# Seven-product tile: ScalarE's four PSUM copies ordered ahead of its casts of later weights

## The chip, the cores and the metric

The kernel runs on one core of one Trainium2 chip. The metric is the device time of one execution in microseconds. Five engines work side by side, each through its own list of instructions in order: TensorE (PE in the profile; its weight loads are shown apart as PEld), VectorE (DVE), ScalarE (ACT), GpSimd (POOL) and SyncE (SP). They wait for each other through semaphores.

## What is computed

The reference is one decoder layer on 512 tokens of width 1024, in float32: a gated feed-forward part, three token mixers (sparse attention, gated delta rule, cross-attention into a memory) whose gated sum is projected, and a second feed-forward part. Cut to what matters here:

```
def swiglu(x, w_gate, w_up, w_down):
    return (jax.nn.silu(x @ w_gate) * (x @ w_up)) @ w_down
...
h = swiglu(rms_norm(x, ffn1_pre_norm[l]), ffn1_w_gate[l], ffn1_w_up[l], ffn1_w_down[l])
x = x + 0.5 * rms_norm(h, ffn1_post_norm[l])
...
gates = jax.nn.sigmoid(u @ w_branch_gate[l]).reshape(b, s, N_BRANCH, d)
merged = (gates[:, :, 0] * (o_nsa @ w_branch_nsa[l]) + gates[:, :, 1] * (o_dn @ w_branch_dn[l]) + gates[:, :, 2] * (o_mem @ w_branch_mem[l]))
...
h = swiglu(rms_norm(x, ffn2_pre_norm[l]), ffn2_w_gate[l], ffn2_w_up[l], ffn2_w_down[l])
```

The feed-forward width is 2816, which makes 22 tiles of 128 features in each feed-forward part.

## The kernel before

**Split products.** A float32 operand is kept as a high part (a cast, on ScalarE) and a low part (operand minus high part, on VectorE). One product is three matmuls: high by high, low by high, high by low.

**The seven-product tile.** One tile needs two products of the same tokens, gate and up, 128 features by 512 tokens each, over 1024 inputs. Seen as a 2 by 2 block matrix (gate and up; two halves of the inputs) times a 2 by 2 block matrix (two halves of the inputs; two halves of the tokens), it takes seven block products in place of eight, at the price of sums of weights and of tokens made beforehand. `fast_prods` (line 469) makes one tile. A block product (`prod`, line 476) is 12 matmuls of 128x256, all from line 482. The seven go into four PSUM banks, called a, q7, g and u in the code. In the profile the banks carry the names smm, so or sr, se, ss in the feed-forward tiles and de, ds, dmm, do in the merge tiles.

**The four copies.** Several results share a partial sum, so ScalarE copies a bank while the tile goes on: after the first product a to the left half of g (line 488), after the third minus a to u (line 493), after the fourth q7 to SBUF (s7, line 495), and after the fifth a to the right half of g (line 497). The third product accumulates on a, so it may not start before the copy of line 488 has read a; the fifth product stands in the same way behind line 493. The names of the seven-product weights S and tokens T pick the block sums. VectorE then makes `up` from s7, a and u (lines 502 and 503), ScalarE the silu of g (line 466) and VectorE the product (line 467).

**The weights of the next tiles.** `fast_load` (line 421) brings the four quarters of a later tile's gate and up weights in by four DMAs on SyncE's queue (tile fq), makes their three sums on VectorE (line 428, tiles fs and fq), seven casts on ScalarE (lines 434 and 441) and the low parts on VectorE (lines 437 and 442). The high and low parts are fset for one set and fxth, fxtl for the other; the sets alternate from tile to tile. The merge has one set (mset, from mfq and msum).

**Where tiles run.** `fast_phase` (line 507) runs 17 tiles in the first feed-forward part (from 75 to 239 us) and 18 in the second (from 1000 to 1173 us). Seven more run in the merge of the mixers (from 774 to 897 us), where cross-attention (lines 1341 to 1361, tiles pms, pmt, pmo) and the products of the branches (pfm) are mixed in. So there are 42 tiles and 168 copies. Beside them ScalarE and VectorE split weights of the down projection ahead of time (line 106 to whi, line 109 to wlo, loaded into wraw by line 105).

**What sets the order.** A scheduler puts every engine's instructions into one fixed list when the kernel is built. It follows priorities, which by default are the order in which the code issues the instructions, and its own estimate of when each can start. `self.tc.high_priority(offset=n)` issues the instructions inside as if they stood n places earlier. Engines then run their lists strictly as written.

Of the kernel before, what the change touches and what calls it, by code (L numbers as in the profile page):

```python
# [14 lines left out]
AF = mybir.ActivationFunctionType  # L15
# [24 lines left out]
class Body:  # L40
# [428 lines left out]
    def fast_prods(self, S, T, banks, s7, mid=()):  # L469

        nc, v, te = self.nc, self.nc.vector, self.nc.tensor
        hi, lo = S
        a, q7, g, u = banks
        a, q7, u = a[:, :256], q7[:, :256], u[:, :256]

        def prod(out, w, t, start=False):
            th, tl = T[t]
            for k in range(4):
                c = slice(k * P, k * P + P)
                wh, wl = hi[:, w, c], lo[:, w, c]  # L480
                n = (k // 2, k % 2) if len(th.shape) == 4 else (k,)
                m = lambda x, y, **kw: te.matmul(out, x, y, skip_group_check=True, **kw)  # L482
                m(wh, th[:, *n], start=start and k == 0, stop=False)
                m(wl, th[:, *n], start=False, stop=False)
                self.tick(m(wh, tl[:, *n], start=False, stop=k == 3), 3 * 256)

        prod(a, self.S_A11, self.T_B11, True)
        nc.scalar.copy(g[:, :256], a)  # L488
        prod(q7, self.S_S3, self.T_T3, True)
        for f in mid[:1]:  # L490
            f()
        prod(a, self.S_S2, self.T_T2)
        nc.scalar.activation(u, a, AF.Copy, scale=-1.0)  # L493
        prod(g[:, :256], self.S_A12, self.T_B21)
        nc.scalar.copy(s7, q7)
        prod(a, self.S_S1, self.T_T1)
        nc.scalar.copy(g[:, 256:], a)  # L497
        prod(u, self.S_A22, self.T_T4)
        for f in mid[1:]:
            f()  # L500
        up = self.tp.tile([P, SEQ], F32, tag="tmpb", bufs=2, name="up")
        v.tensor_tensor(up[:, 256:], s7, a, op=OP.subtract)  # L502
        v.tensor_tensor(up[:, :256], u, s7, op=OP.add)
        prod(g[:, 256:], self.S_S4, self.T_B22)
        return g, up
# [1379 lines left out]
```

## Time and profile before

| | |
|---|---|
| median of 3 runs | 1288.67 us (1288.58 to 1291.4) |
| profiled execution | 1287.24 us |
| its span | 1285.5 us |
| PE busy | 1260.4 us (98%) |
| PEld busy | 1104.8 us (86%) |
| DVE busy | 982.4 us (76%) |
| ACT busy | 733.1 us (57%) |
| granted PE clock | 0.996 of full speed |

A row of the timeline begins with its start and its length in us, then engine, line, operation, output and inputs (buffer numbers left out), and a count where equal instructions follow each other. In brackets stands how long the engine had been idle before and what ended that. A matmul's length is modelled and overlaps the next one; the distance between starts is what counts.

### The profile page before, as it was taken

The numbers are of one execution on the slowest core, as the hardware profiler recorded it, in microseconds if no ns is written. First come the engines' busy times: TensorE is split into PE (matmuls) and PEld (weight loads), VectorE is DVE, ScalarE is ACT, GpSimd is POOL, SyncE is SP. The second block draws the span as 40 slices with busy tenths as digits, with TensorE's granted clock in tenths as the row PEclk, the third lists the DMA queues.
The fourth block names the chain that finished last, engine by engine and source line by source line (L and its number), as shares of the span: only waits on it lengthen the run. The fifth ranks groups of instructions, "written<-read, shape, count | busy, mean of one in ns | idle before, by whom it ended". The sixth has DMA issues, their size and how long they took to land.

```text
span 1285.5 us, 21909 instructions
## 1 busy us (share of the span) xinstructions
PE 1260.4 (98%) x8067; PEld 1104.8 (86%) x8067; DVE 982.4 (76%) x1769; ACT 733.1 (57%) x1487; POOL 209.1 (16%) x224
## 2 busy tenths in 40 slices
PE   8999999999999999999999999999999999999997
PEld 7899999888787778888777778899788999999886
DVE  6898787698967866755789766564797988786988
ACT  6556665675755644415565545553676766655663
POOL 0011112130002222102221112132200121110300
PEclk9999999999999999999999999999999999999999
DMA  6567756894753341233211142132853687664963
GB/s 221 173 200 178 181 165 129 244 210 172 239 186 106 104 125 57 83 111 115 74 58 58 42 146 76 60 112 71 295 192 105 216 183 193 186 130 161 229 224 115
DMA packets 109244, 190.38 MB, mean 148 GB/s; under 512 B 18653, under 2 KB 28241, under 8 KB 109137
## 3 DMA queue, kind: packets, MB, share of 16 engines
q1 hardware_dynamic: 92976, 154.12, 37.2%
q0 software_dynamic: 15872, 34.61, 13.9%
q8 instruction: 63, 1.03, 0.3%
q14 instruction: 45, 0.36, 0.1%
q10 hardware_dynamic: 288, 0.26, 0.1%
HBM read 178.90 MB, written 33.08 MB: 165 GB/s over the span
## 4 chain that ended last, share of the span: by engine, by line
PE 84%; DVE 6%; issue 4%; DMA 3%; ACT 2%; POOL 1%; SPq 0%; ACTq 0%; DVEq 0%; POOLq 0%
PE smm L482 11%; PE se L482 7%; PE acc_mm L712 7%; PE pfm L117 5%; PE pfm L118 5%; PE pfm L119 5%; PE acc_s L712 4%; PE ss L482 4%; PE de L482 2%; PE sr L482 2%; PE ps L1292 2%; PE so L482 2%; PE dmm L482 2%; PE po L1328 1%; PE ppt L1314 1%
## 5 line engine op out<-in xcount | busy, mean ns | idle before, releaser
L106 ACT CAST whi<-wraw 128x512 fp32r<-128x512 f32 (+1 forms) x174 | 105.2, 612 | 108.9 <-PE pfm L119 63.9
L109 DVE TENSOR_TENSOR wlo<-wraw,whi 128x512 fp32r<-128x512 f32 (+1 forms) x142 | 97.3, 694 | 36.3 <-ACT whi L106 34.9
L575 POOL DMA_DIRECT2D T<-in_ffn_d_dram x88 | 59.5, 677 | 380.3 <-PE pg L119 110.7
L118 PE MATMUL pfm<-xth,wlo 128*128 128x512 f32 x272 | 109.0, 406 | 1.3 <-POOL wlo L109 1.3
L117 PE MATMUL pfm<-xth,whi 128*128 128x512 f32 x272 | 108.5, 404 | 1.5 <-ACT whi L106 0.6
L119 PE MATMUL pfm<-xtl,whi 128*128 128x512 f32 x272 | 108.2, 403 | 0.0
L482 PE MATMUL smm<-thi,fset 128*128 128x256 f32 x432 | 76.7, 277 | 0.7 <-ACT ss L493 0.4
L109 POOL TENSOR_TENSOR wlo<-wraw,whi 128x512 fp32r<-128x512 f32 x29 | 39.4, 1361 | 219.7 <-ACT whi L106 165.1
L482 PEld LDWEIGHTS smm<-thi,fset 128*128 128x128 f32 x432 | 65.2, 188 | 1.5 <-ACT se L488 0.7
L502 DVE TENSOR_TENSOR up<-s,smm 128x256 f32<-128x256 f32 x35 | 14.7, 421 | 63.5 <-ACT se L497 63.5
L117 PEld LDWEIGHTS pfm<-xth,whi 128*128 128x128 f32 x272 | 51.2, 189 | 12.3 <-ACT whi L106 1.0
L118 PEld LDWEIGHTS pfm<-xth,wlo 128*128 128x128 f32 x272 | 51.2, 189 | 10.7 <-POOL wlo L109 1.8
L694 ACT CAST ringh<-ringr 128x1024 fp32r<-128x1024 f32 (+1 forms) x44 | 45.1, 1032 | 25.6 <-PE acc_mm L712 7.3
L119 PEld LDWEIGHTS pfm<-xtl,whi 128*128 128x128 f32 x272 | 51.1, 189 | 9.1 <-issue 0.4
L482 PE MATMUL smm<-thi,fxth 128*128 128x256 f32 x204 | 56.3, 276 | 0.0
L482 PE MATMUL smm<-thi,fxtl 128*128 128x256 f32 x204 | 56.3, 276 | 0.0
L482 PE MATMUL se<-thi,fset 128*128 128x256 f32 x288 | 50.9, 276 | 0.0
L727 DVE TENSOR_TENSOR sl<-H,sh 128x1024 fp32r<-128x1024 f32 (+2 forms) x38 | 40.9, 1080 | 4.1 <-ACT sh L726 4.1
L1295 ACT ACTIVATE Pm<-Pm,nm 128x384 f32<-128x384 f32 (+2 forms) x64 | 35.6, 558 | 14.6 <-DVE nm L1294 14.1
L482 PEld LDWEIGHTS se<-thi,fset 128*128 128x128 f32 x288 | 43.4, 188 | 0.0
L428 DVE TENSOR_TENSOR fs<-fq 128x1024 f32<-128x1024 f32 x35 | 43.2, 1233 | 0.0
L712 PE MATMUL acc_mm<-ringh,sh 128*128 128x512 f32 x108 | 42.2, 391 | 0.0
(640 smaller groups left out, 4375.1 us busy)
## 6 DMA issues: line engine op xcount, KB each, us to landing
T<-in_ffn_d_dram POOLq DMA_DIRECT2D x88, 256.0 KB, 4.1
fq<-in_ffn_g_dram SPq DMA_DIRECT2D x70, 256.0 KB, 3.3
fq<-in_ffn_u_dram SPq DMA_DIRECT2D x70, 256.0 KB, 4.0
wraw<-in_ffn_d_dram SPq DMA_DIRECT2D x34, 256.0 KB, 3.7
ringr<-T SPq DMA_DIRECT2D x16, 512.0 KB, 5.0
ringr<-in_ffn_d_dram POOLq DMA_DIRECT2D x16, 512.0 KB, 8.2
woraw<-in_w_out_dram SPq DMA_DIRECT2D x32, 256.0 KB, 3.6
mfq<-in_w_gate_dram SPq DMA_DIRECT2D x28, 256.0 KB, 3.1
```

The costliest lines, as they stand in the source:

```text
L106: nc.scalar.copy(hi, raw)
L109: self.lmark = eng.tensor_tensor(lo, raw, hi.bitcast(F32), op=OP.subtract)
L117: t.matmul(out, lh, rh, start=first, stop=False)
L118: t.matmul(out, ll, rh, start=False, stop=False)
L119: self.tick(t.matmul(out, lh, rl, start=False, stop=last), 3 * math.prod(out.shape[1:]))
L428: add = lambda *x: v.tensor_tensor(*x, op=OP.add)
L482: m = lambda x, y, **kw: te.matmul(out, x, y, skip_group_check=True, **kw)
L575: i = g.dma_start(o[c], x[c], max_dma_last_dim=2048, **({"accum_op": OP.add} if add else {}))
L694: nc.scalar.copy(hi, raw)
L712: e = lambda a, b, s, f: nc.tensor.matmul(acc[i], a, b, start=s, stop=f, skip_group_check=True)
L727: last = tt(low, f, hi.bitcast(F32), op=OP.subtract)
L1295: nc.scalar.activation(pm, pm, AF.Exp, bias=nm[:, qb : qb + 1], scale=-1.0, accum_out=sm[:, qb : qb + 1])
```

## The change

The four copies are issued through a helper that raises their priority by 100 places. Nothing else is altered.

```
+        def first(f, *x, **k):
+            with self.tc.high_priority(offset=100):
+                f(*x, **k)
+
         prod(a, self.S_A11, self.T_B11, True)
-        nc.scalar.copy(g[:, :256], a)
+        first(nc.scalar.copy, g[:, :256], a)
         prod(q7, self.S_S3, self.T_T3, True)
...
         prod(a, self.S_S2, self.T_T2)
-        nc.scalar.activation(u, a, AF.Copy, scale=-1.0)
+        first(nc.scalar.activation, u, a, AF.Copy, scale=-1.0)
         prod(g[:, :256], self.S_A12, self.T_B21)
-        nc.scalar.copy(s7, q7)
+        first(nc.scalar.copy, s7, q7)
         prod(a, self.S_S1, self.T_T1)
-        nc.scalar.copy(g[:, 256:], a)
+        first(nc.scalar.copy, g[:, 256:], a)
```

All four copies now carry the line of the helper's call, 489, and lines behind them are four higher than before. The lists that the scheduler makes are the same but for a few rows. Three places follow.

ScalarE at the first tile of the first feed-forward part, where se is the bank g, smm the bank a, and fxth the casts for the second tile. Before:

```order
L434 CAST fxth<-fq_750 128x512 x3
L441 CAST fxth<-fs 128x512 x2
L441 CAST fxth<-fq_750 128x512
L488 COPY se<-smm 128x256
L495 COPY s_752<-so 128x256
```

And now:

```order
L434 CAST fxth<-fq_750 128x512 x3
L441 CAST fxth<-fs 128x512
L489 COPY se<-smm 128x256
L441 CAST fxth<-fs 128x512
L441 CAST fxth<-fq_750 128x512
L489 COPY s_752<-so 128x256
```

The copy has moved ahead of two casts. On PE, two matmuls of the second tile that stood between the second and the third product of the first tile have gone back to the second tile; and the first tile of the second feed-forward part has its copy ahead of one cast (the second of the two fs) in the same way.

ScalarE in the second tile of the first feed-forward part, from the silu of the first tile on; ss is the bank u. Before:

```order
L466 ACTIVATE sg<-se 128x512
L488 COPY se<-smm 128x256
L434 CAST fxth<-fq_750 128x512
L495 COPY s_753<-sr 128x256
L441 CAST fset<-fq_749 128x512
L493 ACTIVATE ss<-smm 128x256
L441 CAST fxth<-fs 128x512
```

And now:

```order
L466 ACTIVATE sg<-se 128x512
L489 COPY se<-smm 128x256
L434 CAST fxth<-fq_750 128x512
L489 COPY s_753<-sr 128x256
L441 CAST fset<-fq_749 128x512
L441 CAST fxth<-fs 128x512
L489 ACTIVATE ss<-smm 128x256
```

The copy of minus a to u has moved behind one cast.

VectorE at the end of the first tile and in the second; wlo is the low part of a weight of the down projection. Before:

```order
L502 TENSOR_TENSOR up<-s_752,smm 128x256
L109 TENSOR_TENSOR wlo<-wraw,whi 128x512
L442 TENSOR_TENSOR fset<-fs,fset 128x1024
L503 TENSOR_TENSOR up<-ss,s_752 128x256
L437 TENSOR_TENSOR fset<-fq_749,fset 128x1536
L467 TENSOR_TENSOR H<-sg,up 128x512
L428 TENSOR_TENSOR fq_749<-fq_749 128x512
L428 TENSOR_TENSOR fs<-fq_750 128x1024
L442 TENSOR_TENSOR fset<-fq_749,fset 128x1024
L428 TENSOR_TENSOR fq_750<-fs,fq_750 128x512
L502 TENSOR_TENSOR up<-s_753,smm 128x256
```

And now:

```order
L506 TENSOR_TENSOR up<-s_752,smm 128x256
L442 TENSOR_TENSOR fset<-fs,fset 128x1024
L507 TENSOR_TENSOR up<-ss,s_752 128x256
L437 TENSOR_TENSOR fset<-fq_749,fset 128x1536
L467 TENSOR_TENSOR H<-sg,up 128x512
L428 TENSOR_TENSOR fq_749<-fq_749 128x512
L428 TENSOR_TENSOR fs<-fq_750 128x1024
L442 TENSOR_TENSOR fset<-fq_749,fset 128x1024
L428 TENSOR_TENSOR fq_750<-fs,fq_750 128x512
L109 TENSOR_TENSOR wlo<-wraw,whi 128x512
L506 TENSOR_TENSOR up<-s_753,smm 128x256
```

The subtraction wlo has moved back by eight rows. On SyncE's queue the next load of wraw, which needs the buffer that it frees, stands behind four loads of fq now and stood ahead of them before. In the merge, one copy of line 488 stands ahead of one cast, one copy of line 495 behind the cast omth of line 131, and at a few places PE takes tile matmuls and attention matmuls in another alternation. All other rows of all engines stand as before.

## The prediction

> **What bounds the kernel now.** I read the page first, then the list of waits for TensorE (PE) and its weight loads (PEld), then busy time by stage, and last the timeline at the few places where the changed order differs. The page says that PE is busy nearly all of the span:
>
> ```profile
> PE 1260.4 (98%) x8067; PEld 1104.8 (86%) x8067; DVE 982.4 (76%) x1769; ACT 733.1 (57%) x1487; POOL 209.1 (16%) x224
> ```
>
> The change can only help where PE waits for one of the four copies (lines 488, 493, 495, 497). The first two rows are of PE's waits over the whole span, the third of its weight loads between 995 and 1173 us:
>
> ```profile
> PE smm L482 <- ACT ss L493: 0.4, 1, 0.4
> PE smm L482 <- ACT se L488: 0.3, 1, 0.3
> PEld smm L482 <- ACT se L488: 0.2, 1, 0.2
> ```
>
> The columns are total us, times, longest. So 168 copies (four in each of 42 tiles) cost PE three waits. Everywhere else PE does not stop. Busy time by stage (span of the stretch, PE, PEld, DVE, ACT, POOL, clock, DMA share, GB/s), for steady tiles of the first feed-forward part and for the merge:
>
> ```profile
> 92.00:140.00 48.00, 48.00 (x424) 48.00 (x423) 38.62 (x45) 29.91 (x62) 8.45 (x12) 1.00 0.73 176
> 774.00:900.00 126.00, 125.98 (x839) 112.94 (x838) 75.40 (x108) 63.37 (x138) 33.96 (x22) 1.00 0.25 80
> ```
>
> Here a rule has to be weighed. The Trainium skill (Perfetto Trace Analysis, Identifying the Most-Contended Engine) says that matmul occupancy is a bad measure and that weight-load occupancy should be used. By the whole-span PEld figure 14%, about 180 us, would then be open to gain. In the tile stage the trace has 48.00 of 48.00 us for PEld as well, so applied stage by stage the rule leaves nothing there either, and the sum below goes by the three waits.
>
> **The change part by part.** Nothing is added or removed: the same instructions in another order. Of the 168 copies three come earlier by one or two casts, two come later by one, and 163 stand where they stood. I take the places in order of time.
>
> **First tile of feed-forward 1.** PE, around the wait:
>
> ```profile
> 77.12 0.40 PE L482 MATMUL so<-thi,fset 128*128 128x256 f32 x2
> 77.35 0.28 PE L482 MATMUL so<-tmth,fset 128*128 128x256 f32 x1
> 77.47 0.28 PE L482 MATMUL smm<-thi,fxth 128*128 128x256 f32 x1
> 77.59 0.28 PE L482 MATMUL sr<-thi,fxth 128*128 128x256 f32 x1
> 78.16 0.50 PE L482 MATMUL smm<-thi,fset 128*128 128x256 f32 x2 [0.29 <-ACT se L488]
> 78.50 0.28 PE L482 MATMUL smm<-tmth,fset 128*128 128x256 f32 x1
> 78.16 0.30 PEld L482 LDWEIGHTS smm<-thi,fset 128*128 128x128 f32 x2 [0.50 <-ACT se L488]
> ```
>
> Starts are 0.12 us apart (77.35, 77.47, 77.59), so the third product could have started at 77.71; it started at 78.16, 0.45 later. Its first pair then took 0.34 (78.16 to 78.50) where a pair takes 0.23 (77.12 to 77.35): another 0.105. The last row goes with that: the weight load starts with its matmul at 78.16 and not ahead of it. The two matmuls of the next tile at 77.47 and 77.59 filled part of the hole; they are done later now and count neither way. The stall is worth 0.45 + 0.105 = 0.555 us. On ScalarE (ACT):
>
> ```profile
> 76.19 1.14 ACT L441 CAST fxth<-fs 128x512 fp32r<-128x512 f32 x2
> 77.23 0.62 ACT L441 CAST fxth<-fq 128x512 fp32r<-128x512 f32 x1
> 77.75 0.36 ACT L488 COPY se<-smm 128x256 f32<-128x256 f32 x1
> 78.37 1.21 DVE L442 TENSOR_TENSOR fxtl<-fs,fxth 128x1024 fp32r<-128x1024 f32 x1
> ```
>
> Casts follow each other by 0.52 (two in 77.23 - 76.19 = 1.04). In the new order the copy stands behind the first of them: start 76.71, end 77.07, 0.4 before PE wants it at 77.47. The stall is gone in full: bounds 0 and 0.555, I take 0.555. The second fs cast starts about 0.3 later, near 77.0, and ends near 77.6; VectorE (DVE) reads it at 78.37, which hides that.
>
> **Second tile: a copy that comes later.** VectorE's subtraction wlo leaves the first tile, and ScalarE's copy ss now stands behind one cast:
>
> ```profile
> 83.32 0.68 DVE L109 TENSOR_TENSOR wlo<-wraw,whi 128x512 fp32r<-128x512 f32 x1
> 87.66 0.68 DVE L428 TENSOR_TENSOR fq<-fq 128x512 f32<-128x512 f32 x1
> 88.26 1.21 DVE L428 TENSOR_TENSOR fs<-fq 128x1024 f32<-128x1024 f32 x1
> 92.28 0.42 DVE L502 TENSOR_TENSOR up<-s,smm 128x256 f32<-128x256 f32 x1 [1.07 <-ACT se L497]
> 88.37 0.62 ACT L441 CAST fset<-fq 128x512 fp32r<-128x512 f32 x1 [0.19 <-DVE fq L428]
> 89.17 0.37 ACT L493 ACTIVATE ss<-smm 128x256 f32<-128x256 f32 x1 [0.18 <-PE smm L482]
> 89.56 0.62 ACT L441 CAST fxth<-fs 128x512 fp32r<-128x512 f32 x1
> 90.33 0.28 PE L482 MATMUL smm<-thi,fxth 128*128 128x256 f32 x1
> ```
>
> The matmul at 90.33 may not overwrite its bank before ss has read it; it will want to start 0.555 earlier, at 89.775. The cast now ahead of ss needs VectorE's sum fs. Without wlo (a step of 0.60 to the next row in that packed stretch) the sum runs 87.66 to 88.87. A cast starts 0.03 after its VectorE source (87.66 + 0.68 = 88.34 against 88.37), so 88.90; the copy at 89.42, ends 89.79; PE goes on 0.05 after a copy (77.75 + 0.36 = 78.11 against 78.16): 89.84, or 89.90 if the cast starts up to 0.06 later. PE waits 0.07 to 0.12, plus 0.105 for the open weight load if it stops at all. Bounds: 0, and the wait with the sum as late as before, below as a rival. I take +0.2. The displaced wlo falls into the second tile's idle 1.07 us ahead of line 502, which hides its 0.60; without that cover it would cost 0.60 of VectorE, which is idle for a fifth of every steady tile (38.62 of 48.00 busy). The wraw load that it frees goes behind four fq loads on SyncE's queue; its weights are for the down projection, which starts when all tiles are done.
>
> **First tile of feed-forward 2.** The same one-cast move:
>
> ```profile
> 1002.71 0.40 PE L482 MATMUL so<-thi,fset 128*128 128x256 f32 x2
> 1002.95 0.28 PE L482 MATMUL so<-tmth,fset 128*128 128x256 f32 x1
> 1003.24 0.50 PE L482 MATMUL smm<-thi,fset 128*128 128x256 f32 x2
> 1003.58 0.28 PE L482 MATMUL smm<-tmth,fset 128*128 128x256 f32 x1
> 1001.78 1.14 ACT L441 CAST fxth<-fs 128x512 fp32r<-128x512 f32 x2
> 1002.82 0.36 ACT L488 COPY se<-smm 128x256 f32<-128x256 f32 x1
> ```
>
> Due 1003.07, started 1003.24: 0.17, and again 0.105 in the first pair: 0.275. The copy will end at 1002.30 + 0.36 = 1002.66, early enough. Bounds 0 and 0.275, I take 0.275.
>
> **The merge tiles.** A copy of line 488 passes a cast, a copy of line 495 falls behind the cast omth; PE waits for neither (125.98 busy of 126.00), so both are put at nothing; the cover is the branch product that PE runs between second and third product. PE's own order also changes: attention matmuls (pms, pmo) are interleaved with tile matmuls where they stood together, twice. Does a break cost? Four together and two together:
>
> ```profile
> 776.80 1.03 PE L1341 MATMUL pms<-mkT,mq 128*128 128x256 f32 x4
> 777.90 0.28 PE L482 MATMUL de<-ulo,mset 128*128 128x256 f32 x1
> 781.58 0.59 PE L1341 MATMUL pms<-mkT,mq 128*128 128x256 f32 x2
> 782.13 0.59 PE L1341 MATMUL pms<-mkT,mq 128*128 128x256 f32 x2
> ```
>
> Between 776.80 and 777.90 lie four pms and two tile matmuls at 0.117: (1.10 - 0.234) / 4 = 0.217 each. Between 781.58 and 782.13 lie two and one: (0.55 - 0.117) / 2 = 0.217. A break is free: 0, with 0.4 (two breaks at 0.2) as the upper bound.
>
> **The third wait stays.** The wait for ss is in the last tile of feed-forward 1, behind a cast of down weights that waits for its load. No row moves there:
>
> ```profile
> 232.79 1.05 ACT L694 CAST ringh<-ringr 128x1024 fp32r<-128x1024 f32 x1 [0.66 <-DMA ringr<-in_ffn_d_dram]
> 234.16 0.50 PE L482 MATMUL smm<-thi,fset 128*128 128x256 f32 x2 [0.37 <-ACT ss L493]
> ```
>
> **Sum:** -0.555 + 0.2 - 0.275 = -0.63, say -0.6 us, of a profiled execution of 1287.24 us (span 1285.5): 1286.6. That execution lies 1.43 below the median of the runs, 1288.67, from which the forecast is made: **1288.1 us**. A measurement of this kernel can tell about 0.3%, 3.9 us, from no change; this is a sixth of that.
>
> **The rivals.**
> *Nothing arrives.* PE is earlier by half a microsecond at 78 us, but some later stage starts by a transfer that did not move. For it: 1200 us of other work follow. Against: the loads there are released by PE or by buffers that it frees. 1288.67.
> *The removed wait comes back in the second tile.* If the sum fs still ends at 88.26 + 1.21 = 89.47, the cast starts at 89.50 to 89.56, the copy ends at 90.39 to 90.45, PE starts at 90.44 to 90.50 and pays 0.105: 0.22 to 0.28 later than before where I have 0.355 earlier. With the 0.275 of the second feed-forward the total is 0: 1288.6. It decides how far the sum ends after 88.87; each 0.1 us costs 0.1. For it: the row of 234.16 shows just such a chain. The Trainium skill (PSUM — Partial Sum Buffer, Engine vs sequencer instructions) calls ScalarE's queue strictly first-in first-out, and the trace agrees in that row. Against: VectorE's rows there are packed, so taking one out should move the others.
> *Slower: the moved load delays the next tile's weights.* The wraw load (256 KB) goes out some 7 us later, right after the four loads of fq:
>
> ```profile
> 91.06 0.38 SPq L431 DMA_DIRECT2D fq<-in_ffn_u_dram  x1
> 97.17 1.22 DVE L428 TENSOR_TENSOR fs<-fq 128x1024 f32<-128x1024 f32 x1
> fq<-in_ffn_u_dram SPq DMA_DIRECT2D x70, 256.0 KB, 4.0
> ```
>
> At 176 GB/s, 256 KB are 1.5 us. The last fq load should land at 91.06 + 4.0 = 95.1, with the full 1.5 at 96.6, before its sum at 97.17. If the landing slips beyond that, and past the idle time of VectorE, PE loses up to 1.5: 1288.1 + 1.5 = 1289.6.
> *It does not do what it says.* This is largely so: 163 copies do not move. It is in the sum already.
>
> **How the numbers follow.** Chances: forecast 0.60, nothing arrives 0.17, the wait comes back 0.13, slower load 0.05, and 0.05 for something that no row here shows. All named cases lie between 1288.1 and 1289.6, inside 3.9 us of 1288.67: within 0.3% gets 0.95. The last 0.05 is split into 0.02 faster, 0.03 slower. The range takes the cases and the scatter of a run: the profiled execution lay 1.43 under the median, so 1288.1 - 1.4 = 1286.7, to 1286.5 with the bound of no new wait in the second tile (0.2); and 1288.67 + 1.43 = 1290.1 above, which holds the slower case too.
>
> **What would show it.** In the changed profile PE has no wait for line 488's copy in the first tile of either feed-forward, and the third product follows the second by 0.12 us; the one wait for ss near 234 us stays at 0.4; a wait for ss near 90 us is at most 0.15; the first tiles are shorter by 0.5 and 0.3 us, the others as long as they were. Wrong would be: a wait for ss of 0.5 us or more near 90 us, a change of tile length in steady tiles, or a time over 3.9 us from 1288.67.

## The result, and the profile after

The change made the kernel slower: 1300.32 us median of 6 runs (1297.16 to 1302.36) against 1288.71 us of 6 runs before (1288.31 to 1291.40). The ratio is 1.0088, 95% interval 1.0076 to 1.0100, so 9.8 to 12.9 us. The forecast was 1288.1 us with a range of 1286.5 to 1290.1, no change that can be measured. The profiled execution took 1300.86 us, its span 1299.1 us (before 1287.24 and 1285.5), at a granted clock of 0.995.

**The stalls went as forecast.** All of PE's waits for ScalarE's copies, in the list of waits of the changed kernel from 74 to 245 us (total us, times, longest):

```profile
PE smm L482 <- ACT ss L489: 0.2, 1, 0.2
```

From 1000 to 1180 us that list is empty. The timeline of the first tile, PE at the passage from the second to the third product and ScalarE's copy for it:

```profile
78.71 0.40 PE L482 MATMUL so<-thi,fset 128*128 128x256 f32 x2
78.95 0.28 PE L482 MATMUL so<-tmth,fset 128*128 128x256 f32 x1
79.06 0.40 PE L482 MATMUL smm<-thi,fset 128*128 128x256 f32 x2
79.30 0.28 PE L482 MATMUL smm<-tmth,fset 128*128 128x256 f32 x1
79.42 0.40 PE L482 MATMUL smm<-thi,fset 128*128 128x256 f32 x2
79.65 0.28 PE L482 MATMUL smm<-tmth,fset 128*128 128x256 f32 x1
79.77 0.40 PE L482 MATMUL smm<-thi,fset 128*128 128x256 f32 x2
80.01 0.28 PE L482 MATMUL smm<-tmth,fset 128*128 128x256 f32 x1
...
78.30 0.37 ACT L489 COPY se<-smm 128x256 f32<-128x256 f32 x1
```

The copy is done at 78.67, 0.39 us before PE needs it, and the third product follows the second by 0.11 us. The step from one matmul to the next is the same on both sides of that passage: 79.42 to 80.01 are five steps, 0.118 each. Now the rows of the kernel before, directly behind its stall at 78.16:

```profile
78.62 0.39 PE L482 MATMUL smm<-thi,fset 128*128 128x256 f32 x2
78.85 0.28 PE L482 MATMUL smm<-tmth,fset 128*128 128x256 f32 x1
78.97 0.39 PE L482 MATMUL smm<-thi,fset 128*128 128x256 f32 x2
79.19 0.28 PE L482 MATMUL smm<-tmth,fset 128*128 128x256 f32 x1
```

78.62 to 79.19 are also five steps, 0.114 each. Ahead of the stall it was 0.118 (the prediction's rows 77.12 to 77.47 are three steps, 0.117). So the stall of the kernel before ends with a shorter step than it began with, and the changed kernel doesn't get that shorter step here.

**It stays so for the steady tiles.** Busy time by stage for the stretch that the prediction showed, after:

```profile
92.00:140.00 48.00, 48.00 (x410) 48.00 (x409) 38.23 (x46) 29.30 (x59) 8.96 (x12) 1.00 0.70 174
```

Before it was x424 in the same 48.00 us. PE and PEld are busy for the whole of it in both, and the granted clock is 1.00 in both; only the number of matmuls differs. Two longer stretches, one in each feed-forward part, serve as the yardstick for everything that follows. The kernel before:

```profile
110.00:225.00 115.00, 115.00 (x1014) 115.00 (x1013) 91.04 (x106) 69.84 (x142) 19.66 (x28) 1.00 0.65 162
1045.00:1160.00 115.00, 115.00 (x1014) 115.00 (x1013) 91.03 (x106) 69.87 (x142) 20.49 (x29) 1.00 0.69 166
```

The changed kernel:

```profile
110.00:225.00 115.00, 115.00 (x979) 115.00 (x978) 88.98 (x105) 68.94 (x140) 19.00 (x28) 1.00 0.64 161
1045.00:1160.00 115.00, 115.00 (x979) 115.00 (x978) 90.42 (x106) 68.96 (x140) 22.45 (x32) 1.00 0.73 177
```

115.00 us / 1014 is 113.4 ns per matmul, 115.00 / 979 is 117.5: 4.05 ns more. The two parts have 35 tiles of 84 matmuls, 2940 in all, and 2940 x 4.05 ns = 11.9 us. That is a little too much, since some products at the ends of the parts have the same step in both kernels, and the 0.8 us of the two stalls that are gone goes off it. From its first matmul to its last, the first part took 163.7 us before and 168.4 after, the second 172.4 and 178.0: 10.3 us in this pair of profiles, of the 11.6 between the medians. Here the two distances are called the short step and the long step. The expectations below call them the quick and the slow cadence and give them as 113.7 and 117.8 ns. That is the mean distance of starts; the counts give 0.3 less, because a stretch also counts the two or three matmuls that began ahead of it.

**The merge got longer too.** From the first to the last matmul of its seven tiles it took 122.0 us before and 123.4 after. One wait of PE is new there; the list of before is empty from 773 to 900 us (total us, times, longest):

```profile
PE pfm L117 <- DVE tg L1380: 1.0, 1, 1.0
```

and the stage is no longer full:

```profile
780.00:906.00 126.00, 124.95 (x833) 111.94 (x832) 75.13 (x106) 62.40 (x136) 30.79 (x21) 1.00 0.24 77
```

The wait stands at 875.47, and the trace can be followed back from it. The branch product waits for VectorE to read its bank (row tg), VectorE for ScalarE's tanh (tg), ScalarE for a cast ahead of that in its list, and the cast for a weight sum on VectorE (line 428, mfq). That sum takes 1.70 us, where it took 0.68 before. After the change it starts at 871.13, behind GpSimd's subtraction at 870.99; before, it started at 864.75, ahead of GpSimd's at 865.09. The three kernels with the old order of the merge (before, e4 and e8 below) take 122.0 to 122.4 us for this stage and have no such wait; the eleven with the new order take 123.3 to 123.5 and all have it. So the changed order of the merge costs about 1 us. In this pair of profiles it is 1.4, which makes 11.7 us with the two feed-forward parts. (The two executions lie 13.6 apart; 1.6 of that lies ahead of the first tile, where no row has moved.)

### The profile page after: what moved, and what is told of

Same layout as the page of the kernel before. It is cut to its first block, busy times and chain, and to the rows that moved or that the text cites. A ratio compares the mean times of both kernels' runs of the same rounds, so it can differ in the third digit from the quotient of the medians.

```text
span 1299.1 us, 21909 instructions
## 1 busy us (share of the span) xinstructions
PE 1271.9 (98%) x8067; PEld 1116.7 (86%) x8067; DVE 985.7 (76%) x1769; ACT 733.5 (56%) x1487; POOL 207.6 (16%) x224
## 4 chain that ended last, share of the span: by engine, by line
PE 85%; DVE 7%; DMA 3%; ACT 2%; issue 2%; SPq 1%; POOL 0%; DVEq 0%; ACTq 0%
PE smm L482 11%; PE se L482 8%; PE acc_mm L716 7%; PE pfm L117 5%; PE pfm L119 5%; PE pfm L118 5%; PE acc_s L716 4%; PE ss L482 4%; PE sr L482 2%; PE so L482 2%; PE de L482 2%; PE ps L1296 2%; PE po L1332 1%; PE ppt L1318 1%; PE acc_e L716 1%
## 5 line engine op out<-in xcount | busy, mean ns | idle before, releaser
L489 ACT COPY se<-smm 128x256 f32<-128x256 f32 x70 | 25.0, 357 | 50.2 <-PE smm L482 50.1
```

## The experiments

Theory A: the stream of tile matmuls can run at either of two steps and keeps the one it has; which one is decided where the stream starts again after a halt, and the stall that the change removed was what set the short one. Theory B: the moved rows on ScalarE and VectorE make each tile longer. All times are compared with runs of the kernel before on the same chip, since chips differ: its median there was 1292.17 us for e1 to e4, 1290.96 for e5 to e8 and 1286.73 for e9 to e12. One execution of each kernel was profiled, so the counts are those of one execution. The count of matmuls in the two stretches of 115 us tells more than the time: 1013 or 1014 is the short step, 978 or 979 the long one (and 1017 the short one in e8 and e11, where one operand lies otherwise).

| run | ratio to before, 95% interval | 110 to 225 us | 1045 to 1160 us |
|---|---|---|---|
| the change | 1.0088 (1.0076 to 1.0100) | 979 | 979 |
| e1, second part's first tile undone | 1.0062 (1.0028 to 1.0095) | 979 | 979 |
| e5, first part's first tile undone | 1.0044 (1.0023 to 1.0065) | 1013 | 978 |
| e6, both undone, merge changed | 1.0012 (0.9990 to 1.0034) | 1013 | 1014 |
| e2, change, halt at a third product | 1.0003 (0.9986 to 1.0021) | 1013 | 1003 |
| e3, change, halt at a fifth product | 1.0059 (1.0023 to 1.0095) | 1014 | 979 |
| e4, before, halt at a fifth product | 1.0082 (1.0050 to 1.0114) | 978 | 979 |
| e7, change, copies without a halt | 1.0080 (1.0055 to 1.0105) | 979 | 979 |
| e8, before, seventh operand plain | 0.9997 (0.9975 to 1.0019) | 1017 | 1017 |
| e9, change, seventh operand plain | 1.0077 (1.0055 to 1.0099) | 978 | 978 |
| e10, change, break ahead of a third product | 1.0000 (0.9987 to 1.0013) | 1013 | 1013 |
| e11, e10 and e9 together | 1.0000 (0.9982 to 1.0017) | 1017 | 1017 |
| e12, change, break ahead of a second product | 1.0007 (0.9991 to 1.0023) | 1014 | 1013 |

### Undoing the change in parts (e1, e5, e6)

In chosen tiles the copies are issued without raised priority, which puts that tile's old order back. The condition is the one line that differs:

```
         def first(f, *x, **k):
+            if self.plain_tile:
+                return f(*x, **k)
...
+            self.plain_tile = n == 2 and f == f0     # e1; in e5 n == 1 and f == f0; in e6 f == f0
             self.fast_tile(f, self.sets[i], T, banks[i], s7[i], H)
```

e1, expected:

> The change, but the first tile of the second feed-forward part has its copies in the old places again (its row order there is that of before, its PE wait for the first copy comes back). Theory A (the stream of tile matmuls has two cadences, about 117.8 and 113.6 ns from start to start; a halt of PE at the third product of the first tile puts it on the quick one, and it stays there): first part slow at 117.8, second part quick at 113.6, time about 1300.3 - 18 tiles x 0.35 = 1294. Theory B (the cadence follows what ScalarE and VectorE do beside PE in every tile, the halt has no part in it): the steady tiles have the same rows as in the change, so both parts stay at 117.8, about 1300.5.

Measured: 1299.42 us, 7.3 more than before. Only half came as expected. The stall at the first tile of the second part was back and the short step with it, but not for long. PE's timeline in the third tile there (lines are one higher than in the changed kernel):

```profile
1032.00 0.39 PE L483 MATMUL se<-thi,fset 128*128 128x256 f32 x2
1032.23 0.28 PE L483 MATMUL se<-txa,fset 128*128 128x256 f32 x1
1032.34 0.49 PE L483 MATMUL smm<-thi,fset 128*128 128x256 f32 x2
1032.67 0.28 PE L483 MATMUL smm<-txb,fset 128*128 128x256 f32 x1
1032.79 0.40 PE L483 MATMUL smm<-thi,fset 128*128 128x256 f32 x2
1033.02 0.28 PE L483 MATMUL smm<-txb,fset 128*128 128x256 f32 x1
```

1032.00 to 1032.34 are three steps of 0.113. Then the first pair of the fifth product takes 0.33 in place of 0.23, a hitch of 0.1 us, and from 1032.67 on the steps are 0.117. The long step then stays for the 15 tiles that follow, about 5 us. The hitch alone doesn't decide it: the kernel before has the same one at the same product (1025.19 to 1025.52, also 0.33) and keeps the short step behind it.

e5, expected:

> The first tile of feed-forward 1 has its copies in the old order, feed-forward 2 keeps the change. Theory A (the stream of tile matmuls holds one of two cadences, 113.7 or 117.8 ns, and the halt before the third product of the first tile sets the quick one): the halt near 78 us is back, feed-forward 1 runs its 17 tiles at about 113.7 ns, feed-forward 2 has no halt and runs 18 tiles at 117.8. A tile costs 84 x 4.1 ns = 0.345 us more when slow, so about 17 x 0.345 = 5.9 us less than the change as a whole: near 1294.5. Theory B (the displaced work on ScalarE and VectorE makes each tile longer, wherever the first tile's copy stands): as the change, near 1300, both parts at 117.8.

Measured: 1295.72 us, 4.8 more than before. The two stretches:

```profile
110.00:225.00 115.00, 115.00 (x1013) 115.00 (x1013) 92.01 (x108) 70.34 (x143) 19.71 (x28) 1.00 0.65 162
1045.00:1160.00 115.00, 115.00 (x978) 115.00 (x978) 89.07 (x105) 69.91 (x142) 21.50 (x31) 1.00 0.71 172
```

One kernel shows both steps: short in the part whose first tile has its stall back, long in the part without it. Theory A put the long second part at 18 x 84 x 4.05 ns = 6.1 us; the interval is 3.0 to 8.4.

e6, expected:

> Both first tiles of the feed-forward parts have their copies in the old order; all other tiles, the merge's among them, keep the change. Theory A (the halt before the third product sets the quick cadence): both halts are back, both parts run at about 113.7 ns, time within 1.5 us of the kernel before on this chip. Theory B (the moved rows of the other tiles and of the merge cost the time): between 5 and 11 us more than the kernel before, tiles at 117.8 ns.

Measured: 1292.71 us, ratio 1.0012 (0.9990 to 1.0034), 1013 and 1014 matmuls. In the two feed-forward parts ScalarE's and VectorE's rows stand here as before, those of the second tile too; only the merge keeps the change. So the new order of the merge is not what makes the tiles of the parts longer, and the 1 us that it costs in the trace is inside this interval. Theory B keeps its other rows, those moved in the first and the second tile; e10 and e12 below test them.

### A halt put into the changed kernel and into the one before (e2, e3, e4)

Extra copies in the third tile of each part read bank a and write u; they hold the bank so that the third product (e2) or the fifth (e3, e4) must wait. A further line, not shown, keeps the order of PE's list.

```
         prod(a, self.S_A11, self.T_B11, True)
+        for _ in range(3 if self.halt else 0):       # e2
+            first(nc.scalar.copy, u, a)
         first(nc.scalar.copy, g[:, :256], a)
...
         prod(a, self.S_S2, self.T_T2)
+        for _ in range(5 if self.halt else 0):       # e3; in e4 without first
+            first(nc.scalar.copy, u, a)
         first(nc.scalar.activation, u, a, AF.Copy, scale=-1.0)
```

e2, expected:

> The change, with three extra copies of bank a into u (their values are overwritten later, so nothing is computed differently) ahead of the first of the four copies in the third tile of both feed-forward parts; PE has the same list as in the change and must halt there at the third product for 0.4 to 0.9 us. Theory A: tiles 1 and 2 at 117.8 ns, from the halt on 113.6; 30 tiles x 0.35 = 10.5 us gained, 1.3 lost in the halts: about 1291. Theory B: no change of cadence, about 1301.6.

Measured: 1292.37 us, ratio 1.0003 (0.9986 to 1.0021). Busy time by stage, ahead of the halt and behind it:

```profile
80.00:95.00 15.00, 15.00 (x130) 15.00 (x129) 13.90 (x18) 10.54 (x23) 1.77 (x4) 1.00 0.64 205
110.00:225.00 115.00, 115.00 (x1013) 115.00 (x1013) 92.57 (x108) 71.06 (x144) 19.70 (x29) 1.00 0.66 166
```

and the halt between them in PE's timeline:

```profile
98.64 0.40 PE L483 MATMUL so<-thi,fset 128*128 128x256 f32 x2
98.87 0.28 PE L483 MATMUL so<-tmth,fset 128*128 128x256 f32 x1
100.13 0.51 PE L483 MATMUL smm<-thi,fset 128*128 128x256 f32 x2 [0.98 <-ACT se L492]
100.48 0.28 PE L483 MATMUL smm<-tmth,fset 128*128 128x256 f32 x1
100.60 0.39 PE L483 MATMUL smm<-thi,fset 128*128 128x256 f32 x2
```

The kernel got more work and a halt of about a microsecond in each part, and no loss against the kernel before can be measured. In 80 to 95 us it does 130 matmuls as the changed kernel does; behind the halt it runs at the short step up to the last tile of the part. (The 1003 of the second stretch holds one more halt, of 1.2 us, at 1156.47, at a fifth product; the short step came back behind it.)

e3, expected:

> As the run before, but five extra copies ahead of the second of the four copies (minus a into u) in the third tile, so that PE halts at the fifth product for about 1 us. Theory A in its plain form (any halt does it): quick from there, about 1292. Theory A in a narrower form (what PE restarts with decides; in the kernel before a halt at this product in the last tile was followed by 118 ns steps): stays at 117.8, about 1302. Theory B: 1302.

Measured: 1301.44 us. The halt in the first part ended with the long step still there; the short one came 3 us later, at the start of the seventh product of the same tile (105.42 to 105.66 are two steps of 0.12, 105.77 to 106.00 two of 0.115), and stayed:

```profile
105.42 0.40 PE L483 MATMUL se<-thi,fset 128*128 128x256 f32 x2
105.66 0.28 PE L483 MATMUL se<-txb,fset 128*128 128x256 f32 x1
105.77 0.39 PE L483 MATMUL se<-thi,fset 128*128 128x256 f32 x2
106.00 0.28 PE L483 MATMUL se<-txb,fset 128*128 128x256 f32 x1
```

In the second part the long step stayed, but there the granted clock also fell to 0.50 for about 3 us behind the halt, so that this half doesn't stand on the halt alone. The seven runs of e3 spread from 1293.05 to 1304.88 us; whether all of them went as the profiled one did is not shown.

e4, expected:

> The kernel before with the same halt at the fifth product of the third tile. Plain theory A: stays quick, time 1288.7 + 2 = about 1291. If a halt at the fifth product puts the stream on the slow cadence and nothing brings it back: 30 tiles x 0.35 + 2 = about 1301. If the stream finds back to the quick cadence at the seventh product, as it did in the last tile of the first part of before: about 1291. Theory B: about 1291.

Measured: 1301.76 us, ratio 1.0082 (1.0050 to 1.0114). The kernel before, with a halt at the fifth product of the third tile, by stage:

```profile
80.00:95.00 15.00, 15.00 (x134) 15.00 (x133) 13.81 (x18) 10.50 (x21) 1.57 (x3) 1.00 0.66 218
110.00:225.00 115.00, 115.00 (x978) 115.00 (x978) 88.94 (x105) 69.50 (x141) 19.25 (x28) 1.00 0.64 163
```

Short ahead of the halt (134), long behind it. So a halt can lose the short step as well as win it, in a kernel that has none of the change. (In the second part the clock fell to 0.50 behind the halt here too, so the first part is the one that shows it.)

### The same copies without a halt (e7)

```
         first(nc.scalar.copy, g[:, :256], a)
+        for _ in range(3 if self.halt else 0):
+            first(nc.scalar.copy, u, s7)
         prod(q7, self.S_S3, self.T_T3, True)
```

> The change, with three further copies from s7 into the bank u in the third tile of each feed-forward part: the same extra work on ScalarE as in the run with a halt before the third product, but behind the fourth product's copy, where TensorE need not stop for it; TensorE's and VectorE's lists are those of the change. Theory A (only a stop of TensorE can set the quick cadence): no stop, both parts stay at 117.8 ns, within 1.5 us of the change, near 1300. Theory C (work on ScalarE shifted by a microsecond is enough): 113.7 ns from the fourth tile on, near 1291.

Measured: 1300.19 us, ratio 1.0080 (1.0055 to 1.0105):

```profile
110.00:225.00 115.00, 115.00 (x979) 115.00 (x978) 88.97 (x105) 68.87 (x139) 18.87 (x27) 1.00 0.65 160
```

As the change. The copies did not stand where the expectation says: they are issued ahead of the second product, read s7 as an earlier tile left it, and ran at 86.30 us in the second tile, some 11 us earlier than those of e2. PE had no halt there. So three extra copies on ScalarE without a halt of PE do not bring the short step. Since they stood elsewhere, that alone doesn't clear the copies of e2; e10 and e12, which have no extra copies, do.

### The layout of one operand (e8, e9)

In the kernel before, a tile at the short step has a patch of some eight longer steps, from the middle of the sixth product (six of about 118 ns) into the seventh (two of 116). The sixth product's token operand is the only one whose two halves lie apart in memory; it is called stepped here. Both runs lay it out plainly, e8 in the kernel before and e9 in the changed one.

```
-        self.thi = [... for i in range(6)] + [self.stepped(thi[:, 6144:])]
+        self.thi = [... for i in range(7)]
...
-        last = self.stepped(self.cp.tile([P, 1088], F32R, tag="mtl", name="tmtl", bufs=1))
+        last = self.cp.tile([P, 1088], F32R, tag="mtl", name="tmtl", bufs=1)[:, :1024].rearrange("p (k t) -> p k t", k=4)
```

> The kernel before with the seventh token operand (that of the sixth product) laid out plainly, as the other six are, where its two halves stood in steps. Asked is whether that layout makes the patch of 8 or 9 slow steps (117 to 119 ns) in each sixth product of a quick tile. Theory A with the layout as the cause of the patch: the patch goes, tiles at about 113.4 ns throughout, 35 tiles x 8 x 4.4 ns = 1.2 us less than before. The patch has another cause: no difference, within 0.5 us in the profile's tile stages. Third way out: the layout is what keeps the stream able to come back to the quick cadence, and without it the tiles run at 117.8 ns, about 10 us more.

> The change with the seventh token operand laid out plainly. Asked is whether the stepped layout is what holds the changed kernel in the slow cadence. Theory A (the cadence is set where the stream restarts, and nothing restarts it here): both parts stay at 117.8 ns, FFN tile stages of 168.4 and 178.0 us, time as the change, near 1300. Rival (without the layout's slow patch the stream drifts into the quick cadence by itself): 113.3 ns within a few tiles, near 1289.

Measured: e8 0.9997 (0.9975 to 1.0019), e9 1.0077 (1.0055 to 1.0099). By stage, e8:

```profile
110.00:225.00 115.00, 115.00 (x1017) 115.00 (x1016) 91.75 (x108) 70.19 (x142) 19.71 (x28) 1.00 0.66 162
```

and e9:

```profile
110.00:225.00 115.00, 115.00 (x978) 115.00 (x978) 89.77 (x105) 68.36 (x138) 18.82 (x27) 1.00 0.61 158
```

The layout does make the patch, which is gone in e8 (all steps of the sixth product are 113 to 114 ns): 1017 matmuls against 1014, 0.33 ns per matmul, 2940 x 0.33 ns = 1.0 us, too little for the times to show. It does not decide between the two steps: without it the changed kernel stays at the long one.

### A break without a wait (e10, e11, e12)

One further matmul of another shape, 128x512 in place of 128x256, goes into bank u, which is overwritten before anyone reads it. It adds no wait.

```
+        if self.brk:                                  # e10, e11: f == f0; e12: f == f0 + 2, ahead of the second product
+            te.matmul(full, hi[:, 0, :P], T[0][0][:, :2].rearrange("p k t -> p (k t)"), start=True, stop=True, skip_group_check=True)
         prod(a, self.S_S2, self.T_T2)
```

> The change with one further matmul of another shape (128x512, into the bank u, which nobody reads before it is overwritten) ahead of the third product of the first tile in each feed-forward part; no wait is added. Theory A1 (any break of the row of equal matmuls lets the cadence be set anew, and at the third product it comes out quick, at once or with the fourth product as in the merge behind line 119): both parts at 113.7 ns from there, 84 x 4.1 ns = 0.345 us per tile less, 35 tiles: about 12 us less than the change, near 1288.5. Theory A2 (only a stop of TensorE does it): both parts stay at 117.8 ns, near 1300.5.

Measured: 1287.43 us, ratio 1.0000 (0.9987 to 1.0013). PE's timeline at the break (the extra matmul is line 499, the tile's are line 484 here):

```profile
75.38 0.40 PE L484 MATMUL so<-thi,fset 128*128 128x256 f32 x2
75.61 0.28 PE L484 MATMUL so<-tmth,fset 128*128 128x256 f32 x1
75.73 0.39 PE L499 MATMUL ss<-thi,fset 128*128 128x512 f32 x1
75.96 0.39 PE L484 MATMUL smm<-thi,fset 128*128 128x256 f32 x2
76.19 0.28 PE L484 MATMUL smm<-tmth,fset 128*128 128x256 f32 x1
76.31 0.39 PE L484 MATMUL smm<-thi,fset 128*128 128x256 f32 x2
76.53 0.28 PE L484 MATMUL smm<-tmth,fset 128*128 128x256 f32 x1
```

75.38 to 75.73 are three steps of 0.117; the extra matmul takes 0.23; 75.96 to 76.53 are five steps of 0.114. By stage the short step holds in both parts:

```profile
110.00:225.00 115.00, 115.00 (x1013) 115.00 (x1012) 90.90 (x107) 68.47 (x139) 19.71 (x29) 1.00 0.62 159
1045.00:1160.00 115.00, 115.00 (x1013) 115.00 (x1013) 91.00 (x106) 69.23 (x142) 20.49 (x29) 1.00 0.67 164
```

So two extra matmuls, 0.46 us of work in all, take back what the change lost in the two parts; the new wait in the merge is still there, and its 1 us is inside the interval. It needs no stop of PE; a break in the row of equal matmuls is enough. The rows that the change moved in the second tile stand moved in this kernel too.

> The two edits together: the break ahead of the third product of each first tile, and the seventh token operand laid out plainly. By theory A1: 113.3 ns in all tiles but the start of the first, tile stages of 163.0 and 171.4 us plus what the last tile of the first part loses, 1 to 2 us less than the kernel before, 1287 to 1288 on a chip where that takes 1288.7. By theory A2: 117.8 ns, near 1300.5.

Measured: 1286.79 us, ratio 1.0000 (0.9982 to 1.0017), with 1017 matmuls in both stretches. The microsecond that the plain layout saves lies inside the interval: this version is as good as the kernel before, and is not shown to be better.

> The change with the same further matmul ahead of the second product of the third tile in each feed-forward part: the same break at another place. If every break comes out quick: two tiles at 117.8 ns, then 113.7, near 1289.5. If the place decides (third product quick, elsewhere not): 117.8 ns throughout, near 1300. If it is open at this place, as it is in the merge behind tile pmo (there both are seen), one part may go one way and the other the other: near 1295. Theory A2 (only a stop does it): 117.8 ns throughout.

Measured: 1288.84 us, ratio 1.0007 (0.9991 to 1.0023). By stage, ahead of the break and behind it:

```profile
80.00:95.00 15.00, 15.00 (x130) 15.00 (x129) 13.90 (x18) 9.75 (x20) 1.57 (x3) 1.00 0.65 223
110.00:225.00 115.00, 115.00 (x1014) 115.00 (x1013) 91.32 (x107) 70.14 (x142) 19.66 (x28) 1.00 0.64 162
```

A break ahead of the second product brings the short step too, in both parts. ScalarE's and VectorE's rows stand in the order of the change throughout, so all rows that it moved are still moved, and the short step is back. Theory B falls here.

## Why the prediction was wrong

**What bounds the kernel.** Right as far as it went: PE has no idle time in the steady feed-forward tiles, before or after. The prediction then took "48.00 of 48.00 us" to mean that nothing can change there. That is the gap: the same full 48.00 us hold 424 matmuls or 410. Weight loads tell no more than matmuls, 48.00 of 48.00 in both kernels. The passage of the Trainium skill that the prediction weighs (Perfetto Trace Analysis, Identifying the Most-Contended Engine) names two measures, the matmul work done in the window against the peak and the busy share of weight loads; the prediction took only the second, and a count of the work done is what tells the two kernels apart here. The Trainium skill (TensorE: Matmul & The Clock Gate, Back-to-back issue gap) gives, for a stream of weight loads and matmuls, one sustained distance at each of the widths 128 and 512, and none for 256. The trace has two for 256, 113.4 and 117.5 ns at a granted clock of 1.00, and it goes before a reading with one.

**The stalls, -0.555 and -0.275.** Right: both are gone, and the copy is ready 0.39 us early, where 0.4 was forecast.

**The second tile, +0.2.** It was not called on: PE has no wait there. The copy came about as late as forecast, counted from the start of the first tile, but at the long step PE reaches the fifth product of the second tile some 0.4 us later than the sum assumed. In e10, with the short step, one step there takes 0.14 in place of 0.11.

**The merge, 0.** Too small: it cost about 1 us, above the bound of 0.4. The prediction asked whether the moved copies and the interleaved matmuls cost PE anything where they stand, and put both at nothing. The new wait comes from elsewhere, from a sum on VectorE that now runs behind GpSimd's subtraction and holds up a cast, a tanh and then PE. Which of the moved rows shifts VectorE against GpSimd there was not tested.

**The wait for ss that stays.** Right: it is there, at 0.2 us in place of 0.4.

**The step that failed** is the sum itself, in the words of the prediction: "the first tiles are shorter by 0.5 and 0.3 us, the others as long as they were". It priced a stall by its length, as something that is only ever lost. This stall also left PE at another step than it found it, and 35 tiles ran on that: the term for the other tiles was put at nothing, and it measured 10.3 us net of the stalls that are gone. The two numbers that show the two steps stood in the prediction's own rows: steps of 0.12 us ahead of the stall (77.35, 77.47, 77.59) and 48.00 us / 424 = 113.2 ns behind it. They were not set side by side. The second term that failed is the merge's, put at nothing where it cost about 1 us. Of the prediction's marks for being wrong, "a change of tile length in steady tiles" came, and with it the time over 3.9 us away.

**The rivals.** None was this one. All of them moved single waits and so lay within 1.5 us; the case came out of the 0.05 left for something that no row shows, of which 0.03 was put on slower.

**What is shown and what is open.** Shown: the loss is the longer step in the two feed-forward parts (count of matmuls, clock unchanged); it goes with the missing stall (e5, e6) and not with the moved rows, which are all still there in e12 at the short step; a halt or a mere break brings the short step back (e2, e10, e12) and a halt in the kernel before can take it away (e4). The 1 us in the merge is shown too, by the kernels that have its new order, e6 with nothing else changed among them; the chain that leads to it is read from the traces and not tested. Open: why a fresh start gives one step or the other. At the second and third product all 18 halts and breaks in the feed-forward tiles of the fourteen profiles, those at 78.16 and 1003.24 among them, led to the short one. At the fifth product both came: of 25 halts and hitches at full clock the short step followed 17 and the long one 8 (in the changed kernel the one wait left, near 240 us, ended in the short step; e4 at 102.42 in the long). The first product of each part always began with the long one, though matmuls of another shape stand ahead of it, so a break does not bring the short step everywhere. Why the sixth product's layout costs long steps without deciding the rest is open as well.

## What to carry to other kernels

When an engine is full in both profiles, count its instructions in equal stretches, or take the distance of starts, and compare ahead of and behind each stall: full does not mean equally fast. A stall of half a microsecond can be worth ten if the stream behind it runs in another rhythm, so before removing one, look at whether the step changes across it. Where it does, try a cheap break (here one extra matmul of another shape, 0.23 us) in its place, and judge by the count, not by the time alone. And compare every stage that has a changed order from its first instruction to its last, also where the moved rows themselves seem to cost nothing.

## What the runs showed of the hardware

A row of 128x256 matmuls, each with its own weight load, held one of two steps for up to 18 tiles on end: 113.4 or 117.5 ns by the count, at a granted clock of 1.00. It changed between them at hitches of 0.1 us (e1 at 1032.34) as well as at halts of a microsecond (e2), at one matmul of another shape (e10, e12), and four times at the start of a seventh product without either (e3 at 105.42; before at 237.10; e1 and e7 near 243). A stepped operand cost 1.0 us over 2940 matmuls in the kernel with the short step. VectorE's sum mfq in the merge (128x512) took 0.68 us where it started 0.2 to 0.3 us ahead of a subtraction on GpSimd (before, e4, e8) and 1.4 to 1.8 us where it started up to 0.4 us behind it (the eleven others).
